# Mixer input normalised once, its products copied out by ScalarE, and the low part of the mixer's weights made in VectorE's stream beside its chains

## The chip, the cores and the metric

The kernel runs on one core of a Trainium2 chip. The metric is the device time of one execution in microseconds. The time before is 1730.99 us, the median of three runs (1728.68 to 1732.05). The profile shows one execution with a span of 1730.2 us.

## The reference

One decoder layer for 512 prompt tokens and 32 sample tokens (8 sequences of 4), 544 rows in all, in float32:

```python
x = x + 0.5 * swiglu(rms(x, norm_ffn1), w_ffn1_gu, w_ffn1_down)     # 1024 -> 2 x 2816 -> 1024
h = rms(x, norm_mix)
qa, ka, va, qkv_b, z_b, b_b, a_b, gate = split(h @ w_in)            # 3 x 1536, 3072, 1024, 8, 8, 2048
o_a, kv_rows = dilated_window_attention(qa, ka, va, caches)         # 12 heads, 3 groups, merged to 4 x 128
o_b, conv_new, s_new = gated_deltanet(qkv_b, z_b, b_b, a_b, ...)    # conv of width 4, 8 heads, chunks
gt = sigmoid(gate)
x = x + (gt[:, :1024] * (o_a @ w_proj_a) + gt[:, 1024:] * (o_b @ w_proj_b)) @ w_out
x = x + 0.5 * swiglu(rms(x, norm_ffn2), w_ffn2_gu, w_ffn2_down)
y = rms(x, norm_out)

def rms(x, w): return x * rsqrt(mean(x * x) + 1e-6) * w
```

The new keys and values, the conv state and the delta-rule state are outputs as well.

## The kernel before

Activations lie transposed: 128 features on the partitions, 544 tokens in two halves of 272 along the row (`NH`). Every large product runs in three passes of a reduced float32: a weight tile is split into a high part (`G`, a rounded copy) and a low part (what the rounding left), the activations likewise (`xh` and `xl`), and hi x hi, hi x lo and lo x hi are summed in PSUM. A *unit* is one 128-column tile of a weight matrix for one half of the tokens; it has eight (or 4, or 11) weight tiles, 24 matmuls of 272 columns. `make_plan` lists all 458 units in order: first feed-forward, the mixer's input projection (`ba`, `gdn`, `at`, `z`, `gate`, 154 units), output projections (`pa`, `pb`, `wo`), second feed-forward.

Before a unit, `prefetch` (L457) lets `split_next` (L424) bring weight tiles in, four at a time: ScalarE makes the high part, and the low part is a subtraction on VectorE or GpSimd. In the mixer it is GpSimd unless the unit's kind is in `LOV`. Four such groups have a place, that is two columns of tiles: while one column is used by its two halves, the next is made. The raw weights come by DMA into two buffers, issued in the mixer from GpSimd's queue (`load_raw`, L401). After a unit's matmuls `kernel_units` (L650) issues its evacuation: the product lies in one of three PSUM banks (`mm`) and must be copied out before the third unit after it.

A norm's weight is multiplied in before the split (`xw_tile`), but a token's 1/rms is not: it is known late, and each evacuation multiplies the product by it (`R(h)`, a tile per half). In `u_gdn`, `u_at`, `u_z` and `u_gate` this is a VectorE product of PSUM and `r`; for two of the three attention groups it also reorders the tokens by residue (strided).

Beside the units run *side chains*, Python generators: the conv (`conv`), the delta-rule pairs (`gdn_pair`), attention slots and so on. Between the matmuls of a unit `pump` (L616) issues the next step of every chain that seems ready. It judges this by `Meter` (L46), an estimate of when each engine gets through what it was given. So the order on every engine is fixed when the program is built, and each engine's queue runs in order. On the chip a VectorE instruction of a chain and an evacuation wait for each other only by their place in that queue.

Tiles come from a pool of 62 (`S`); a chain waits, in the order of issue, until it has enough.

Of the kernel before, what the change touches and what calls it, by code (L numbers as in the profile page):

```python
# [10 lines left out]
F32 = mybir.dt.float32  # L11
F32R = mybir.dt.float32r
# [25 lines left out]
CFG = dict(S=62, S2=4, G=4, G2=8, RAW=2, U3=3, H=10, HM=6, LA=4, LAG=3.0, SLACK=0.0, BANKS=3, PRE=3, LOV=("pa", "pb"), CV=0, WARM=4, EP=8, DUE=2, RES=0, RQ="gpsimd")  # L38
# [87 lines left out]
class Plan:  # L126
    """Order in which the 128 x 128 weight tiles are used; host and chip follow it."""
# [76 lines left out]
def consts():  # L204
    """Arrays that depend on shapes alone: identity, masks and distances."""
# [53 lines left out]
class Builder:  # L259
# [30 lines left out]
    def until(self, ok):  # L290
        """The side chains go on until something holds."""
# [96 lines left out]
    def rsqrt(self, out, v, tmp, steps):  # L388
        """out = v ** -0.5 by a shifted exponent and Newton steps."""
# [34 lines left out]
    def split_next(self, ui, pool=None):  # L424
        """Bring the next group of weight tiles in as hi + lo if a slot is free."""
# [121 lines left out]
    def xw_tile(self, n, h, which):  # L547
        """x * w as hi + lo; the tokens' 1/rms is applied to the products."""
# [9 lines left out]

    def norm_fin(self, h):
        """1/rms of one half of the tokens, on all partitions."""  # L560
# [6 lines left out]
        self.r[h] = self.sp.tile([P, NH], F32, tag="r", name=self.nm("r"), bufs=2)  # L567
# [31 lines left out]
    def step(self, g):  # L599
        """One step of a side chain; it says what its next step waits for."""  # L600
# [15 lines left out]
    def pump(self):  # L616
        """Issue what the side chains have ready."""
# [116 lines left out]

    def enter_mix(self):
# [4 lines left out]
        self.in_mix = True  # L740
        self.live = 16 + 1 + 2 + KT
# [28 lines left out]
    def u_z(self, n, h, wids):  # L770
# [6 lines left out]
        def evac():  # L777
# [5 lines left out]
            self.tt(z, ps, self.R(h), ALU.mult)  # L783
            self.act(t, z, AF.Tanh, scale=0.5)
# [3 lines left out]
    def z_fin(self, n, h, z, t):  # L788
        """A head's output, gated, as hi + lo."""
# [13 lines left out]
    def z_load(self, n):  # L803
        """The output of head n, once it is there."""
# [8 lines left out]
    def fin_a(self):  # L813
        """The attention's heads as hi + lo."""
# [18 lines left out]

    def u_gdn(self, hd, t, h, wids):
        nc = self.nc
        ps = self.unit(wids, self.xn, h)

        def evac():
            ct = t * 8 + hd
            if h == 0:  # L840
# [6 lines left out]
                self.tt(U[:, 3:275], ps, self.R(h), ALU.mult)  # L847
# [3 lines left out]
            self.tt(U[:, 275:515], ps[:, :240], self.R(h)[:, :240], ALU.mult)  # L851
# [942 lines left out]
```

## Time and profile before

| what | value |
|---|---|
| median of the runs | 1730.99 us |
| span of the profiled execution | 1730.2 us |
| TensorE busy | 1656.1 us (96%) |
| VectorE busy | 1072.3 us (62%) |
| ScalarE busy | 573.1 us (33%) |
| GpSimd busy | 373.4 us (22%) |
| chain that ended last | TensorE 73%, VectorE 20%, DMA 3%, ScalarE 2% |

The mixer's units stand at about 415 to 1150 us. In rows of the profile PE is TensorE, DVE VectorE, ACT ScalarE, POOL GpSimd. `mm` and `sd` are PSUM tiles of units and side chains (outside the mixer units use both). Matmuls are pipelined, so a busy PE need not be at its peak. Nearly all instructions carry the line of one helper (L120), so groups are told apart by their tiles' names: `G` weights, `raw` weights as loaded, `U` and `y` input and output of the conv, `av` a projected attention head, `smp` its sample rows, `r` the 1/rms, `Yc`, `Uc` and `inv` a chain's triangular solve, `R` its decay.

### The profile page before, as it was taken

To read this page: it belongs to the slowest core of one execution; us is meant where nothing else is said; L and a number is where in the kernel's file an instruction comes from. 1 tells how busy PE (TensorE), PEld (TensorE's weight loads), DVE (VectorE), ACT (ScalarE), POOL (GpSimd) and SP (SyncE) were. 2 spreads that over 40 slices of the span, in tenths; PEclk is the share of its full clock that TensorE was granted. 3 is DMA by queue.
4 is the path that set the end of the run, shared out by engine and by line. 5 is a ranking of instruction groups with operands and counts; after the bars stand their busy time and mean duration, and the time that the engine had idled before them with its cause. 6 is when DMAs were issued, how large, how long until landed. Compare 5 with 4: busy or idle time off the path is not lost.

```text
span 1730.2 us, 33573 instructions
## 1 busy us (share of the span) xinstructions
PE 1656.1 (96%) x13373; PEld 1607.8 (93%) x13373; DVE 1072.3 (62%) x2508; ACT 573.1 (33%) x1356; POOL 373.4 (22%) x441
## 2 busy tenths in 40 slices
PE   8999999999988999999899899999999999999997
PEld 7999999999988888888889788999999999999996
DVE  7754255545879869789958665344456654255534
ACT  5332223332332324343333244333233323223332
POOL 5000000011545534454425233420011000000012
PEclk9999999999999999999999999999999999999999
DMA  5223222322333455446347666332243222223221
GB/s 177 87 85 98 86 86 86 98 85 75 111 100 115 135 180 185 135 156 193 117 137 238 171 219 182 123 119 89 86 139 97 84 89 87 97 74 98 86 75 63
DMA packets 116434, 205.13 MB, mean 119 GB/s; under 512 B 30962, under 2 KB 57108, under 8 KB 116276
## 3 DMA queue, kind: packets, MB, share of 16 engines
q1 hardware_dynamic: 104708, 162.43, 29.2%
q0 software_dynamic: 10992, 39.99, 7.7%
q8 instruction: 105, 1.72, 0.4%
q10 hardware_dynamic: 576, 0.56, 0.1%
q14 instruction: 53, 0.43, 0.1%
HBM read 172.20 MB, written 30.73 MB: 117 GB/s over the span
## 4 chain that ended last, share of the span: by engine, by line
PE 73%; DVE 20%; DMA 3%; ACT 2%; issue 2%; SPq 1%; POOL 0%; DVEq 0%; ACTq 0%
PE sd L120 40%; PE mm L120 32%; DVE y L120 4%; DVE Yc L120 3%; DVE inv L120 2%; DVE H L120 1%; DVE nrm L120 1%; DVE ast L120 1%; DVE av L120 1%; DVE s L120 1%; DVE R L120 1%; DMA md<-ast 1%; DVE U L120 1%; DVE kq L120 1%; DVE r L120 1%
## 5 line engine op out<-in xcount | busy, mean ns | idle before, releaser
L120 PE MATMUL mm<-xh,G 128*128 128x272 f32 x3632 | 753.7, 297 | 21.6 <-DVE smp L120 10.4
L120 PEld LDWEIGHTS mm<-xh,G 128*128 128x128 f32 x3632 | 596.6, 192 | 42.5 <-issue 26.5
L120 PE MATMUL mm<-xl,G 128*128 128x272 f32 x1816 | 530.0, 292 | 0.5 <-DVE xl L120 0.4
L120 PE MATMUL sd<-xh,G 128*128 128x272 f32 x1904 | 363.4, 288 | 0.0
L120 PEld LDWEIGHTS mm<-xl,G 128*128 128x128 f32 x1816 | 349.2, 192 | 1.4 <-DVE xl L120 0.6
L120 ACT ACTIVATE G<-raw 128x512 fp32r<-128x512 f32 x474 | 273.3, 619 | 178.6 <-PE mm L120 111.6
L120 PEld LDWEIGHTS sd<-xh,G 128*128 128x128 f32 x1904 | 300.5, 188 | 0.2
L120 POOL TENSOR_TENSOR G<-raw,G 128x512 fp32r<-128x512 f32 x158 | 217.3, 1391 | 322.7 <-ACT G L120 303.0
L120 PE MATMUL sd<-xl,G 128*128 128x272 f32 x952 | 273.8, 288 | 0.0
L120 DVE TENSOR_TENSOR G<-raw,G 128x512 fp32r<-128x512 f32 x316 | 204.7, 690 | 70.9 <-ACT G L120 66.7
L120 POOL TENSOR_TENSOR acc<-acc,H 128x272 f32<-128x272 f32 x55 | 44.7, 814 | 911.5 <-ACT H L120 908.1
L120 PEld LDWEIGHTS sd<-xl,G 128*128 128x128 f32 x952 | 179.0, 188 | 0.1
L120 PE MATMUL sd<-hh,G 128*128 128x272 f32 x1287 | 163.0, 288 | 0.0
L120 PEld LDWEIGHTS sd<-hh,G 128*128 128x128 f32 x1287 | 161.8, 188 | 0.1
L120 ACT ACTIVATE H<-H 128x272 f32<-128x272 f32 (+1 forms) x105 | 45.1, 429 | 193.4 <-DVE H L120 193.4
L120 ACT ACTIVATE hh<-H 128x272 fp32r<-128x272 f32 x88 | 38.0, 431 | 202.0 <-DVE H L120 202.0
L120 PE MATMUL mm<-hh,G 128*128 128x272 f32 x825 | 104.7, 288 | 0.0
L120 PEld LDWEIGHTS mm<-hh,G 128*128 128x128 f32 x825 | 103.8, 188 | 0.0
L120 DVE SCALAR_TENSOR_TENSOR y<-U,vec,y 128x568 f32<-128x568 f32 x72 | 94.2, 1308 | 7.8 <-ACT y L120 6.0
L120 DVE SCALAR_TENSOR_TENSOR H<-H,H 128x272 f32<-128x272 f32 x120 | 55.2, 460 | 26.3 <-ACT H L120 25.8
L120 DVE SCALAR_TENSOR_TENSOR x<-sd,x 128x272 f32<-128x272 f32 x49 | 21.4, 439 | 77.9 <-PE sd L120 77.9
L120 DVE TENSOR_TENSOR hh<-H,hh 128x272 fp32r<-128x272 f32 x88 | 38.9, 442 | 43.8 <-ACT hh L120 43.8
(257 smaller groups left out, 1853.3 us busy)
## 6 DMA issues: line engine op xcount, KB each, us to landing
raw<-in_W_dram SPq DMA_DIRECT2D x161, 512.0 KB, 3.6
raw<-in_W_dram POOLq DMA_DIRECT2D x76, 512.0 KB, 4.0
qkv<-qd SPq DMA_DIRECT2D x36, 256.0 KB, 5.4
st<-in_ssm_dram SPq DMA_DIRECT2D x32, 256.0 KB, 4.5
cache<-in_kc_dram SPq DMA_DIRECT2D x28, 256.0 KB, 5.2
cache<-in_vc_dram SPq DMA_DIRECT2D x28, 256.0 KB, 4.3
qd<-av SPq DMA_DIRECT2D x24, 256.0 KB, 4.2
out_dram<-av SPq DMA_DIRECT2D x24, 256.0 KB, 3.8
```

The lines of the kernel that those rows point to most:

```text
L120: r = f(*args, **kw)
```

## The change

`LOV` now has every kind of unit, so all low parts of the mixer are VectorE subtractions. The 1/rms of both halves lies in one tile `rr`. When the second half's is there, a side chain `renorm` makes x * w * r for eight tiles and splits it anew into `xh` and `xl`. From the eleventh unit of the mixer on (`NORMED` = 10) the units use these, and their products need no factor, so `take` copies them out with ScalarE. `u_z` and `u_gate` take ScalarE for their products throughout. The spill of the residual waits for `renorm`. (Docstrings and comments also go, which moves line numbers by two: L120 is L122.)

```diff
-CFG = dict(..., LOV=("pa", "pb"), ...)
+NORMED = 10
+CFG = dict(..., LOV=("pa", "pb", "ba", "z", "gate", "gdn", "at"), ...)
...
+    def renorm(self):
+        ts = []
+        def finish():
+            t, (hi, lo) = ts.pop(0), self.xn2[-1 - len(ts)]
+            self.tt(lo, t, hi, ALU.subtract)
+            self.free(1)
+        for n in range(KT):
+            yield from self.need(3)
+            t = self.S(name="xt")
+            self.stt(t, self.x[n], self.wn[1][:, n:n + 1], self.rr, ALU.mult, ALU.mult)
+            if ts:
+                finish()
+            yield "scalar"
+            self.xn2.append((self.S(dt=F32R, name="xh"), self.S(dt=F32R, name="xl")))
+            self.act(self.xn2[-1][0], t, AF.Copy)
+            ts.append(t)
+            t = None
+            yield "vector"
+        finish()
+        self.renormed = True
...
-        self.r[h] = self.sp.tile([P, NH], F32, tag="r", name=self.nm("r"), bufs=2)
+        if h == 0:
+            self.rr = self.sp.tile([P, NT], F32, tag="r", name=self.nm("r"), bufs=1)
+        self.r[h] = self.rr[:, self.sl(h)]
...
+        elif h == 1 and self.in_mix:
+            self.spawn(self.renorm())
...
             self.prefetch(ui)
+            if ui == first_ba + NORMED:
+                self.until(lambda: self.renormed)
+                self.xn, self.xn2, self.normed = self.xn2, None, True
+                self.free(2 * KT)
...
-            self.tt(z, ps, self.R(h), ALU.mult)
-            self.act(t, z, AF.Tanh, scale=0.5)
+            self.act(t, ps, AF.Tanh, scale=0.5)
+            self.act(z, ps, AF.Copy)
...
+    def take(self, out, ps, r, done):
+        if done:
+            self.act(out, ps, AF.Copy)
+        else:
+            self.tt(out, ps, r, ALU.mult)
...
-                self.tt(U[:, 3:275], ps, self.R(h), ALU.mult)
+                self.take(U[:, 3:275], ps, self.R(h), done)
...
-            self.tt(self.smp[:, t, j, g, :], ps[:, 240:272], self.R(h)[:, 240:272], ALU.mult)
+            self.take(self.smp[:, t, j, g, :], ps[:, 240:272], self.R(h)[:, 240:272], done)
...
-            self.tt(t, ps, self.R(h), ALU.mult)
-            self.act(t, t, AF.Tanh, scale=0.5)
+            self.act(t, ps, AF.Tanh, scale=0.5)
```

On VectorE, at the first `gdn` units of the mixer, stands before (`U` is a unit's product on its way into the conv, `LB` and `LA` the decay's inputs, `y` the conv):

```order
457 L120 TENSOR_TENSOR U_4762<-mm_4737,r_4633 128x272
458 L120 COPY LB_4778<-sd_4773 128x32
459 L120 COPY LA_4779<-sd_4773 128x32
460 L120 TENSOR_TENSOR U_4762<-mm_4766,r_4720 128x240
461 L120 TENSOR_TENSOR U_4762<-mm_4766,r_4720 128x8x4
462 L120 SCALAR_TENSOR_TENSOR y_4816<-U_4762,vec_79,y_4816 128x568 x3
463 L120 MEMSET U_4856 128x3
464 L120 COPY U_4856<-convout_4653 128x8x3
465 L120 TENSOR_TENSOR U_4856<-mm_4826,r_4633 128x272
```

and now:

```order
459 L122 TENSOR_TENSOR U_4760<-mm_4735,r_4632 128x272
460 L122 SCALAR_TENSOR_TENSOR xt_4768<-x_71,vec_79,r_4632 128x544
461 L122 COPY LB_4778<-sd_4773 128x32
462 L122 COPY LA_4779<-sd_4773 128x32
463 L122 TENSOR_TENSOR U_4760<-mm_4764,r_4632 128x240
464 L122 TENSOR_TENSOR U_4760<-mm_4764,r_4632 128x8x4
465 L122 SCALAR_TENSOR_TENSOR xt_4811<-x_72,vec_79,r_4632 128x544
466 L122 TENSOR_TENSOR xl_4801<-xt_4768,xh_4800 128x544
467 L122 TENSOR_TENSOR G_4818<-raw_4460,G_4818 128x512
468 L122 TENSOR_TENSOR G_4821<-raw_4460,G_4821 128x512
469 L122 SCALAR_TENSOR_TENSOR y_4816<-U_4760,vec_79,y_4816 128x568 x3
```

Two subtractions of `G` now stand between two columns' evacuations, and a pair of `xt` and `xl` between a few of the chain's instructions.

On VectorE, a dozen units later, at the first attention head, stands before (`kq`, `scat` and `vT` are the conv's results):

```order
523 L120 TENSOR_TENSOR U_5213<-mm_5217,r_4720 128x8x4
524 L120 TENSOR_TENSOR av_5285<-mm_5259,r_4633 128x272
525 L120 SCALAR_TENSOR_TENSOR kq_5208<-U_5116,y_5223 128x256
526 L120 SCALAR_TENSOR_TENSOR kq_5209<-U_5116,y_5223 128x256
527 L120 SCALAR_TENSOR_TENSOR scat_4656<-U_5116,y_5223 128x32
528 L120 SCALAR_TENSOR_TENSOR y_5292<-U_5213,vec_79,y_5292 128x568 x3
529 L120 TENSOR_TENSOR av_5285<-mm_5294,r_4720 128x240
530 L120 TENSOR_TENSOR smp_4657<-mm_5294,r_4720 128x32
531 L120 SCALAR_TENSOR_TENSOR vT_5350<-U_5213,y_5292 128x512
```

and now:

```order
548 L122 MEMSET U_5266 128x3
549 L122 COPY U_5266<-convout_4652 128x8x3
550 L122 TENSOR_TENSOR G_5298<-raw_5086,G_5298 128x512
551 L122 TENSOR_TENSOR G_5301<-raw_5086,G_5301 128x512
552 L122 SCALAR_TENSOR_TENSOR kq_5119<-U_5173,y_5228 128x256
553 L122 SCALAR_TENSOR_TENSOR kq_5120<-U_5173,y_5228 128x256
554 L122 SCALAR_TENSOR_TENSOR scat_4655<-U_5173,y_5228 128x32
555 L122 SCALAR_TENSOR_TENSOR y_5315<-U_5266,vec_79,y_5315 128x568 x3
556 L122 TENSOR_TENSOR G_5371<-raw_5236,G_5371 128x512
557 L122 TENSOR_TENSOR G_5374<-raw_5236,G_5374 128x512
558 L122 SCALAR_TENSOR_TENSOR vT_5387<-U_5266,y_5315 128x512
```

The copies of `av`, `smp` and `U` are gone from between the conv's instructions, and a pair of `G` has come before every new column.

On ScalarE at the same place stands before:

```order
319 L120 ACTIVATE y_5223<-U_5116,vec_79 128x568
320 L120 ACTIVATE G_5251<-raw_5077 128x512
321 L120 ACTIVATE G_5254<-raw_5077 128x512
322 L120 ACTIVATE U_5116<-y_5223 128x568
323 L120 ACTIVATE y_5292<-U_5213,vec_79 128x568
324 L120 ACTIVATE G_5325<-raw_5180 128x512
325 L120 ACTIVATE G_5328<-raw_5180 128x512
326 L120 ACTIVATE U_5213<-y_5292 128x568
```

and now:

```order
332 L122 ACTIVATE U_5173<-y_5228 128x568
333 L122 ACTIVATE U_5266<-mm_5270 128x240
334 L122 ACTIVATE U_5266<-mm_5270 128x8x4
335 L122 ACTIVATE G_5298<-raw_5086 128x512
336 L122 ACTIVATE G_5301<-raw_5086 128x512
337 L122 ACTIVATE y_5315<-U_5266,vec_79 128x568
338 L122 ACTIVATE av_5338<-mm_5306 128x272
339 L122 ACTIVATE av_5338<-mm_5340 128x240
340 L122 ACTIVATE smp_4656<-mm_5340 128x32
341 L122 ACTIVATE G_5371<-raw_5236 128x512
342 L122 ACTIVATE G_5374<-raw_5236 128x512
343 L122 ACTIVATE U_5266<-y_5315 128x568
```

The evacuations have come into ScalarE's queue, each behind whatever the chains put there, such as the `tanh` (`U` from `y`) that waits for VectorE's three `y`.

## Rows read from the trace of the kernel before

**Rows 1.** Table of stretches: us, busy time of each engine, granted clock, DMA share, GB/s.
```profile
414.00:600.00 186.00, 166.38 (x1249) 161.86 (x1249) 154.17 (x381) 56.02 (x153) 88.92 (x102) 0.94 0.34 110
600.00:800.00 200.00, 188.08 (x1608) 173.51 (x1607) 165.38 (x461) 76.97 (x218) 87.53 (x111) 0.98 0.56 174
800.00:1000.00 200.00, 183.63 (x1628) 167.75 (x1626) 153.57 (x450) 63.31 (x177) 81.31 (x98) 0.97 0.52 163
1000.00:1107.00 107.00, 101.89 (x872) 93.01 (x873) 58.31 (x153) 42.12 (x113) 36.70 (x40) 0.97 0.61 188
```

**Rows 2.** Waits of TensorE, 414 to 1107 us: us in total, times, longest.
```profile
PE mm L120 <- DVE smp L120: 10.4, 3, 5.1
...
PE sd L120 <- DVE nrm L120: 1.1, 1, 1.1
```

**Rows 3.** The chain that ended last: its shares in 414 to 1107 us, and one piece.
```profile
by line: PE mm L120 22.6%; PE sd L120 17.1%; DVE y L120 9.7%; DVE Yc L120 7.0%; DVE inv L120 6.1%; issue 3.8%; DVE nrm L120 2.7%; DVE ast L120 2.3%; DVE av L120 2.1%; DVE s L120 1.9%; DVE R L120 1.9%; DMA md<-ast 1.8%; DVE U L120 1.8%; DVE 
...
1107.14 38.41 PE mm L120 x306
```

**Rows 4.** Timeline of VectorE: start, us, instruction, how many merged, idle before.
```profile
420.84 0.76 DVE L120 SCALAR_TENSOR_TENSOR xl<-x,vec,xh 128x272 fp32r<-128x272 f32 x1 [0.97 <-ACT xh L120]
...
434.11 4.32 DVE L120 SCALAR_TENSOR_TENSOR y<-U,vec,y 128x568 f32<-128x568 f32 x3 [0.90 <-ACT y L120]
...
528.93 0.42 DVE L120 TENSOR_TENSOR Yc<-Yc,inv 128x248 f32<-128x248 f32 x1
...
533.49 1.70 DVE L120 TENSOR_TENSOR Yc<-Yc,inv 128x224 f32<-128x224 f32 x1
...
664.75 2.49 DVE L120 SCALAR_TENSOR_TENSOR y<-U,vec,y 128x568 f32<-128x568 f32 x3
...
1089.52 0.78 DVE L120 TENSOR_TENSOR ol<-H,oh 128x272 fp32r<-128x272 f32 x1 [0.78 <-ACT oh L120]
```

**Rows 5.** Timeline of GpSimd from 533 us.
```profile
533.65 2.66 POOL L120 TENSOR_TENSOR G<-raw,G 128x512 fp32r<-128x512 f32 x2
```

**Rows 6.** Groups of the whole span: busy us, mean ns, idle before.
```profile
L120 PE MATMUL mm<-xh,G 128*128 128x272 f32 x3632 | 753.7, 297 | 21.6 <-DVE smp L120 10.4 <-ACT G L120 5.2 <-DVE av L120 3.2
...
L120 DVE TENSOR_TENSOR G<-raw,G 128x512 fp32r<-128x512 f32 x316 | 204.7, 690 | 70.9 <-ACT G L120 66.7
...
L120 POOL TENSOR_TENSOR G<-raw,G 128x512 fp32r<-128x512 f32 x158 | 217.3, 1391 | 322.7 <-ACT G L120 303.0 <-PE sd L120 19.3
...
L120 DVE SCALAR_TENSOR_TENSOR y<-U,vec,y 128x568 f32<-128x568 f32 x72 | 94.2, 1308 | 7.8 <-ACT y L120 6.0
```

**Rows 7.** ScalarE's group for the weights' high part, 414 to 1107 us.
```profile
L120 ACT ACTIVATE G<-raw 128x512 fp32r<-128x512 f32 x138 | 80.8, 621 | 77.7 <-PE mm L120 65.4 <-DMA raw<-in_W_dram 4.5 <-issue 3.5
```

**Rows 8.** VectorE's groups of product copies, whole span.
```profile
L120 DVE TENSOR_TENSOR av<-mm,r 128x272 f32<-128x272 f32 x36 | 20.4, 567 | 5.3 <-issue 2.8 <-PE mm L120 2.4
...
L120 DVE TENSOR_TENSOR av<-mm,r 128x240 f32<-128x240 f32 x36 | 18.7, 520 | 7.7 <-PE mm L120 7.7
...
L120 DVE TENSOR_TENSOR U<-mm,r 128x272 f32<-128x272 f32 x24 | 10.4, 433 | 1.6 <-PE mm L120 1.6
...
L120 DVE TENSOR_TENSOR U<-mm,r 128x240 f32<-128x240 f32 x24 | 9.5, 397 | 5.9 <-PE mm L120 5.9
...
L120 DVE TENSOR_TENSOR gate<-mm,r 128x272 f32<-128x272 f32 x22 | 9.7, 440 | 36.9 <-PE mm L120 36.9
...
L120 DVE TENSOR_TENSOR smp<-mm,r 128x32 f32<-128x32 f32 x36 | 6.5, 182 | 0.0
```

**Rows 9.** ScalarE's copies out of PSUM, by width.
```profile
L120 ACT ACTIVATE pT<-sd 128x384 f32<-128x384 f32 x8 | 3.9, 486 | 8.5 <-PE sd L120 8.4
...
L120 ACT ACTIVATE vn<-sd 128x512 f32<-128x512 f32 x12 | 7.1, 593 | 11.8 <-PE sd L120 11.5
```

**Rows 10.** Waits of ScalarE for VectorE, 414 to 1107 us.
```profile
ACT U L120 <- DVE y L120: 44.0, 14, 4.2
...
ACT ast L120 <- DVE ast L120: 26.5, 4, 9.8
```

More of the change, by code (lines that the diff above doesn't have):

```diff
@@ L36 @@
 C_KA, C_VA, C_QKV, C_Z, C_B, C_A, C_GATE = 1536, 3072, 4608, 7680, 8704, 8712, 8720
-CFG = dict(S=62, S2=4, G=4, G2=8, RAW=2, U3=3, H=10, HM=6, LA=4, LAG=3.0, SLACK=0.0, BANKS=3, PRE=3, LOV=("pa", "pb"), CV=0, WARM=4, EP=8, DUE=2, RES=0, RQ="gpsimd")
+NORMED = 10
+CFG = dict(S=62, S2=4, G=4, G2=8, RAW=2, U3=3, H=10, HM=6, LA=4, LAG=3.0, SLACK=0.0, BANKS=3, PRE=3, LOV=("pa", "pb", "ba", "z", "gate", "gdn", "at"), CV=0, WARM=4, EP=8, DUE=2, RES=0, RQ="gpsimd")
 MIX_ORDER = [("p", 0), ("p", 1), ("a", 0), ("p", 2), ("a", 1), ("p", 3), ("a", 2), ("a", 3), ("p", 4), ("a", 4), ("p", 5), ("a", 5)]
@@ L654, in kernel_units @@
         pend = []
+        first_ba = next(i for i, u in enumerate(self.units) if u[0] == "ba")
         for ui, u in enumerate(self.units):
             self.prefetch(ui)
+            if ui == first_ba + NORMED:
+                self.until(lambda: self.renormed)
+                self.xn, self.xn2, self.normed = self.xn2, None, True
+                self.free(2 * KT)
             pend.append(getattr(self, "u_" + u[0])(*u[1:]))
@@ L832, in fin_a @@
             self.split(hl[0][:, NPR:NT], hl[1][:, NPR:NT], self.smo[:, 32 * j:32 * j + 32])
+    def take(self, out, ps, r, done):
[3 more added lines that the diff above has]
+            self.tt(out, ps, r, ALU.mult)
     def u_gdn(self, hd, t, h, wids):
-        nc = self.nc
+        nc, done = self.nc, self.normed
         ps = self.unit(wids, self.xn, h)
@@ L850, in evac @@
             us = U[:, 515:571].rearrange("p (b s) -> p b s", s=7)
-            self.tt(U[:, 275:515], ps[:, :240], self.R(h)[:, :240], ALU.mult)
+            self.take(U[:, 275:515], ps[:, :240], self.R(h)[:, :240], done)
             b4 = lambda a: a.rearrange("p (b s) -> p b s", s=4)
-            self.tt(us[:, :, 3:7], b4(ps[:, 240:272]), b4(self.R(h)[:, 240:272]), ALU.mult)
+            self.take(us[:, :, 3:7], b4(ps[:, 240:272]), b4(self.R(h)[:, 240:272]), done)
             self.spawn(self.conv(U, hd, t, self.convs[1]))
@@ L902, in spill @@
         self.xd = self.D([P, KT, NT], "xd")
+        while not self.renormed:
+            yield "w"
         while self.x:
@@ L1362, in u_at @@
     def u_at(self, j, g, t, h, wids):
-        nc, A = self.nc, self.A
+        nc, A, done = self.nc, self.A, self.normed
         ps = self.unit(wids, self.xn, h)
@@ L1372, in evac @@
             if g == 0:
-                self.tt(self.av.rearrange("p a b -> p (a b)")[:, lo:lo + w], ps[:, :w], r, ALU.mult)
+                self.take(self.av.rearrange("p a b -> p (a b)")[:, lo:lo + w], ps[:, :w], r, done)
             else:
                 rn = lambda a: a.rearrange("p (n r) -> p r n", r=4)
-                self.tt(self.av[:, :, lo // 4:(lo + w) // 4], rn(ps[:, :w]), rn(r), ALU.mult)
+                self.take(self.av[:, :, lo // 4:(lo + w) // 4], rn(ps[:, :w]), rn(r), done)
             if h == 0:
                 return
-            self.tt(self.smp[:, t, j, g, :], ps[:, 240:272], self.R(h)[:, 240:272], ALU.mult)
+            self.take(self.smp[:, t, j, g, :], ps[:, 240:272], self.R(h)[:, 240:272], done)
             hd = 4 * g + j
```

1 line of the change is left out of this document (added).

## The prediction

> **What bounds the kernel now.** I read the page first, then a table of stretches, the waits of TensorE, the chain that ended last, and a timeline of VectorE and GpSimd. TensorE is busy nearly always, but its idle time is not spread evenly. In the mixer's part from 414 to 1107 us, 693 us long, four rows of the table [rows 1] give TensorE 640.0 us busy, so 53 us idle. Their granted clock, weighted by length, is 0.965. TensorE's clock has two levels, 1.2 and 2.4 GHz, so 0.965 means that 7% of the 693 us, some 48 us, ran at the lower one, which costs half of that, 24 us. These 53 + 24 = 77 us are what a change to the other engines could win here. It is a little too low, since a matmul counts as busy for 0.297 us [rows 6] though the next may start earlier: each stop hides some tenths.
>
> VectorE is the engine behind this. It is busy 154.2 + 165.4 + 153.6 + 58.3 = 531 us of the 693 [rows 1], 81% up to 1000 us. TensorE's longest waits name its copy of a product (`smp`, up to 5.1 us at once) [rows 2]; twelve such lines of waits for VectorE, from 10.4 to 1.1 us, come to 36 of the 53 us. On the chain that ended last, VectorE's named shares for this stretch (y, Yc, inv, nrm, ast, av, s, R, U) add up to 35.5%, or 246 us [rows 3].
>
> Much of VectorE's time there is not work. Three `y` instructions in a row took 4.32 us in one place and 2.49 in another [rows 4]. A `Yc` that starts at 533.49 takes 1.70 us and lies over two subtractions of `G` that GpSimd runs from 533.65 on [rows 5]; one at 528.93, a little larger and with no such neighbour, takes 0.42 [rows 4]. I compared every VectorE instruction between 414 and 1107 us that a GpSimd subtraction of `G` overlaps with the median of its own kind outside such an overlap (the strided `av` left aside). 101 of them were longer by over 0.15 us, by 95 us in all; the first (`xl`) and the last (`ol`) stand in [rows 4].
>
> The Trainium skill, SBUF — State Buffer, section "Who interferes with whom", says that a VectorE instruction with two SBUF inputs and a GpSimd instruction that reads SBUF lock each other out for a whole instruction. By that rule all 95 us go with the subtractions; if 4.32 us were simply what three `y` cost, none would (rival C).
>
> **The change part by part**, for 414 to 1107 us.
>
> 1. Low part of the weights off GpSimd. 152 subtractions move from GpSimd, where one takes 1.39 us, to VectorE, where one takes 0.690 [rows 6]. 138 of them lie in this stretch (ScalarE's high parts, one for each, are counted there in [rows 7]), which is +95 us for VectorE. What the 101 instructions lose to such overlaps goes: -95 us. `zm`, `kn` and `vk` stay on GpSimd, so a little overlap stays. GpSimd's own time was off the path and wins nothing.
>
> 2. Products copied by ScalarE. VectorE loses 36 + 36 `av` (20.4 + 18.7 us), 36 `smp` (6.5), 20 of 24 `U` pairs (10.4 + 9.5 us, so 16.6, and 20 small third ones at `smp`'s 0.18, 3.6), 32 `gate` and, of the same size, 16 `H` at 0.44 (21.1) [rows 8]: 87 us, of which 7 are gates beside the output projections, where TensorE never waits. That leaves -80 us. ScalarE gains some 60: a 272-wide copy out of PSUM is not in the trace, but 384 columns take 0.486 us and 512 take 0.593 [rows 9], so 272 is about 0.39 on the same line. For the strided `av` I know no ScalarE row; the bounds are 0.39 and VectorE's ratio for it (0.567 as a mean against 0.433 for `U`), so 0.39 to 0.51. I take 0.42, nearer to the first, since a third of the `av` are not strided. ScalarE is busy 238 us of the 693 [rows 1], so it has room by sum.
>
> The Trainium skill, ScalarE: Activation LUTs, section "Rules for kernel authors", speaks against this step: it wants simple arithmetic on VectorE rather than ScalarE. Here both need about 0.4 us for such a tile, so by the rows the move is free where ScalarE has room; by the rule it would be a loss on ScalarE, which nothing in this stretch is bound by.
>
> 3. The normalised input. Eight `xt` (a two-input instruction over 544 columns; `y` over 568 is 2.49 / 3 = 0.83 without an overlap, so 0.80) and eight `xl` (0.690 at 512, so 0.73): 8 x 1.53 = +12 us on VectorE, plus eight copies on ScalarE. All must be done before the eleventh unit of the mixer. Until then TensorE has ten units of 24 matmuls, which at 38.41 us for 306 in a row [rows 3] is 30 us, and VectorE's queue now holds, by the order, eight `xt`/`xl` pairs, ten `G`, four to five `y` triples and the first copies: roughly 12 + 7 + 11 + 8 = 38 us. I count the 12 us as lying fully on the path. The residual's spill (SP queue) starts some 30 us later and is needed only after the mixer: nothing. Sixteen more tiles are held till then, which delays the first delta-rule pair by a few units; by the order the last side matmuls stand before the same unit as now, so I take nothing.
>
> 4. New queues. A copy now stands in ScalarE's queue behind side work that waits for VectorE (`U<-y`, then `U<-mm`), and VectorE's `G` stands behind ScalarE's `G`, which waits for TensorE to let go of a slot: 65 us in all [rows 7]. A weight slot and a PSUM bank are both wanted two units, 6 us, later, so most of these waits are covered; what they cost if not is rival A. GpSimd's raw loads now wait for VectorE instead of GpSimd, a pair of units ahead: nothing.
>
> VectorE's sum is -95 - 80 + 95 + 12 = -68 us: 463 instead of 531. On time, I count each term by how much of it lies on the chain. `y` is the largest part of the 95 us, and 67 of its 94 us are on the chain (9.7% of 693, [rows 3, 6]), so -95 x 0.7 = -66. Copies on the chain: `av` 2.1% and `U` 1.8%, -27. `G` on VectorE only counts while VectorE is the chain: 246 of 531, so 95 x 0.46 = +44. `xt`/`xl` +12. Together -37. The lower clock came after such stops; if half of it goes, -12. The total is -49 us. The span of the profiled execution is 1730.2, the median of the runs 1730.99, 0.8 above; 1731 - 49 = 1682 us.
>
> **Rivals.**
> - A, slower: ScalarE's queue becomes the serial path. Everything that TensorE wants next (weights' high part, then through VectorE the low part, and the emptied bank) stands behind ScalarE's waits for VectorE. In the trace these are long (`U` for `y` 44.0 us, `ast` for `ast` 26.5 with one of 9.8 [rows 10]), and 9.8 is over the 6 us of cover. For it: two engines must now be on time instead of one of three. Against it: these waits are for instructions that the overlaps stretched. If these 44 + 26.5 = 70 us stay and 70% of them reaches TensorE, the 49 us are gone, and from there on the kernel is slower; if all 70 do, the time is 1731 - 49 + 70 = 1752.
> - B, little won: what bounds is then the next thing on the chain, DMA round trips and the order. `md`'s round trip alone holds 1.8% of the chain, 12 us [rows 3], and the order, not readiness, places the side matmuls. If these take two thirds of the 49, 1715. For it: from 1000 to 1107 us VectorE is 54% busy, and the granted clock is 0.97 there too [rows 1]. Against it: only a seventh of the stretch is like that.
> - C, the change doesn't do what it says, as the long `y` have another cause: VectorE then has -80 + 95 + 12 = +27 us, and the path -27 + 44 + 12 = +29: 1760. [Rows 4, 5] speak against it: same instruction, same sizes, 0.83 and 1.44 us each.
> - D, more: VectorE falls so far (67%) that TensorE hardly waits, and the 77 us nearly all go: 1655.
>
> **How the numbers follow.** The forecast, with its own range of 1660 to 1705, has 0.55; D 0.17; B 0.16; A 0.08; C 0.04. The range has to hold 8 in 10: from 1645 (D, with some of the hidden tenths per stop) up to 1720 (most of B); outside are A and C and a rest of B and D. About 0.2% is what a measurement of this kernel can tell from no change, here 3.5 us. Faster by more: 0.55 + 0.17 + most of B = 0.84. Within it: 0.04, out of B. Slower: A and C, 0.12.
>
> **What the profile of the changed kernel would show.** Right: three `y` at about 2.5 us everywhere, and VectorE's `G` at 0.69; VectorE busy near 463 us in the mixer, which is then near 645 us long; the lines "PE mm <- DVE smp" and "<- DVE av" gone; a stop of up to some 12 us before the eleventh unit; a granted clock of 0.98 or more. Wrong: waits of TensorE for VectorE's or ScalarE's `G`, or for ScalarE's `av`, of tens of us (A); `y` still near 1.3 us on average (C); VectorE under 70% busy but TensorE idle for DMA (B). The stretch up to 414 us and that after the mixer should keep their lengths within 2 us.

## The result, and the profile after

The changed kernel takes 1716.7 us (median of 4 runs, 1715.5 to 1718.3) beside 1731.5 for the kernel before on the same chip. The ratio on record is 0.990, 95% interval 0.988 to 0.992 (the two medians alone give 0.991). It is faster by 15 to 17 us: inside the range, but the forecast was 49. The profiled execution spans 1716.5 us.

First the two places in which the forecast's mechanism is to be seen. These are groups of the whole span, columns as in [rows 6]:

```profile
L122 PE MATMUL mm<-xh,G 128*128 128x272 f32 x3632 | 744.3, 296 | 9.0 <-ACT xh L122 3.1
...
L122 DVE TENSOR_TENSOR G<-raw,G 128x512 fp32r<-128x512 f32 x468 | 303.9, 691 | 180.3 <-ACT G L122 174.7
...
L122 DVE SCALAR_TENSOR_TENSOR y<-U,vec,y 128x568 f32<-128x568 f32 x72 | 62.1, 863 | 3.8 <-ACT y L122 1.9
```

`y` fell from 1308 ns to 863 [rows 6], and VectorE's `G` kept its 691, as forecast. The chain's shares from 414 us to the end of the side work (1095 us now) say the same, beside [rows 3]:

```profile
by line: PE mm L122 48.4%; PE sd L122 21.6%; DVE R L122 2.6%; DMA md<-ast 2.4%; DVE y L122 2.3%; issue 2.3%; DMA ob<-od 1.7%; DVE G L122 1.7%; DMA st<-in_ssm_dram 1.5%; DMA cache<-in_kc_dram 1.3%; ACT s L122 1.1%; DVE H L122 0.8%; DMA ast<-
```

VectorE has nearly left the chain: `y` 2.3% where it was 9.7, `Yc` and `inv` gone from the part of the list that is shown. TensorE holds 70% of it. Yet the time hardly moved. The stretches, beside [rows 1], with two short ones below them:

```profile
414.00:600.00 186.00, 169.54 (x1278) 164.62 (x1277) 141.91 (x395) 74.54 (x217) 31.37 (x63) 0.94 0.38 120
600.00:800.00 200.00, 185.96 (x1618) 169.03 (x1617) 147.04 (x444) 87.69 (x267) 35.34 (x70) 0.95 0.54 167
800.00:1000.00 200.00, 187.65 (x1679) 175.20 (x1677) 132.07 (x409) 79.29 (x243) 30.92 (x62) 0.97 0.56 174
1000.00:1107.00 107.00, 103.04 (x866) 95.40 (x867) 58.33 (x178) 48.59 (x138) 11.41 (x19) 0.94 0.57 177
...
450.00:478.00 28.00, 15.18 (x70) 12.79 (x69) 19.99 (x55) 8.01 (x17) 3.95 (x6) 0.63 0.12 39
...
985.00:1010.00 25.00, 14.35 (x118) 12.72 (x118) 15.28 (x46) 4.45 (x12) 4.81 (x6) 0.59 0.64 176
```

VectorE is busy 479 us of the 693 (531 before, 463 forecast). TensorE is idle 47 us instead of 53, and its mean granted clock fell from 0.965 to 0.951. The last two rows show where: in two stops, 53 us together, TensorE is busy 29.5 us at a mean clock of about 0.6. Its waits from 414 to 1095 us, beside [rows 2]:

```profile
PE mm L122 <- DVE xl L122: 8.5, 5, 4.5
PE sd L122 <- DVE X L122: 8.4, 2, 8.0
...
PE mm L122 <- ACT xh L122: 3.1, 2, 1.8
```

VectorE's `smp` and `av` are gone from this list, as forecast. `xl`, the low part of the normalised input, and one `X` of 8.0 us head it, and its high part `xh` stands in it too. **The first stop** is the eleventh mixer unit, the first on the normalised input. TensorE there (start us, us, instruction, idle before and its releaser):

```profile
453.45 0.39 PE L122 MATMUL mm<-xl,G 128*128 128x272 f32 x1 [0.66 <-DVE xl L122]
...
455.77 0.39 PE L122 MATMUL mm<-xh,G 128*128 128x272 f32 x1 [1.80 <-ACT xh L122]
460.69 0.59 PE L122 MATMUL mm<-xl,G 128*128 128x272 f32 x1 [4.53 <-DVE xl L122]
...
467.40 0.60 PE L122 MATMUL mm<-xl,G 128*128 128x272 f32 x1 [2.80 <-DVE xl L122]
...
469.80 1.87 PE L122 MATMUL sd<-g,mats 128*128 128x32 f32 x8 [1.57 <-DVE g L122]
```

and VectorE's timeline, which has no gap longer than 0.7 us from 440 to 470 us:

```profile
457.91 1.29 DVE L122 TENSOR_TENSOR G<-raw,G 128x512 fp32r<-128x512 f32 x2
...
459.22 0.78 DVE L122 SCALAR_TENSOR_TENSOR xt<-x,vec,r 128x544 f32<-128x544 f32 x1
459.92 0.72 DVE L122 TENSOR_TENSOR xl<-xt,xh 128x544 fp32r<-128x544 f32 x1
...
463.42 2.50 DVE L122 SCALAR_TENSOR_TENSOR y<-U,vec,y 128x568 f32<-128x568 f32 x3
...
466.63 0.72 DVE L122 TENSOR_TENSOR xl<-xt,xh 128x544 fp32r<-128x544 f32 x1
```

The eight `xt`/`xl` pairs are spread among `G`, `y` and the decay's small steps, and each `xl` is awaited at once. From the start of its first matmul to the start of its last the unit takes 21.1 us, in the kernel before 5.9, a stop of 15 us in all. From 456 to 477 us TensorE runs at the lower of its two clocks (1.2 GHz): the mean of 0.63 over the 28 us means 21 us of it.

**The second stop** is at the first z units. The first z unit begins at 976.4 us, before at 1021.5, 45 us later. Not all of this is a lead. Here are TensorE's side matmuls (`sd`) from 414 us to the first z unit and from there to the projections, first of the kernel before, then of the changed one (us, busy time and count, granted clock, DMA share, GB/s):

```profile
414.00:1021.50 607.50, 185.69 (x1727) 0.97 0.48 149
1021.50:1148.30 126.80, 23.96 (x247) 0.97 0.54 166
...
414.00:976.40 562.40, 160.12 (x1513) 0.96 0.48 151
976.40:1136.40 160.00, 51.44 (x460) 0.93 0.55 169
```

Some 26 us of side work have only been put behind the first z unit. And the z units need the heads, while the last delta-rule pair has just reached its level stage, which joins the blocks of its triangular solve (`X,B`, `Y,Pm`, `Y,Q`). From 982.6 to 1004.2 us the order holds nothing but side matmuls. TensorE:

```profile
988.91 0.77 PE L122 MATMUL sd<-zm,kf 128*128 128x512 f32 x1
997.71 1.94 PE L122 MATMUL sd<-X,B 128*64 128x64 f32 x16 [8.03 <-DVE X L122]
...
1003.14 1.08 PE L122 MATMUL sd<-cache,pT 128*32 128x128 f32 x16 [0.84 <-DMA cache<-in_vc_dram]
1004.15 0.60 PE L122 MATMUL mm<-xh,G 128*128 128x272 f32 x1
```

and VectorE, which is to make that `X`:

```profile
985.42 1.29 DVE L122 TENSOR_TENSOR G<-raw,G 128x512 fp32r<-128x512 f32 x2 [4.61 <-ACT G L122]
...
988.33 2.57 DVE L122 SCALAR_TENSOR_TENSOR H<-H,H 128x272 f32<-128x272 f32 x1
995.63 0.44 DVE L122 TENSOR_TENSOR H<-H,ob 128x272 f32<-128x272 f32 x1 [4.74 <-DMA ob<-od]
...
997.26 0.30 DVE L122 STREAM_TRANSPOSE X<-Y 32x128 f32<-32x128 f32 x1
```

VectorE stands for 4.7 us at a z unit's product with a head (`ob`) that is still on its way from DRAM, and the `X` that TensorE wants lies behind it. The `H` before it took 2.57 us where the same instruction takes 0.43 at 995.99. It lies over three `zm` that GpSimd still makes: some 2 of the 8 us are what is left of the overlaps.

```profile
987.55 3.03 POOL L122 TENSOR_TENSOR zm<-stk,mats 128x512 fp32r<-128x512 f32 x3
...
995.99 0.43 DVE L122 SCALAR_TENSOR_TENSOR H<-H,H 128x272 f32<-128x272 f32 x1
```

When the projections begin (1136.5 us against 1148.4), 12 of the 45 us are left: 26 were side work put off, and the rest, 7, is about what the stop cost.

### The profile page after: what moved, and what is told of

It reads as the page before. It is cut to its first block, busy times and chain, and to the rows that moved or that the text cites. A ratio compares the mean times of both kernels' runs of the same rounds, so it can differ in the third digit from the quotient of the medians.

```text
span 1716.5 us, 33595 instructions
## 1 busy us (share of the span) xinstructions
PE 1648.8 (96%) x13373; PEld 1603.2 (93%) x13373; DVE 1010.2 (59%) x2460; ACT 618.8 (36%) x1548; POOL 169.0 (10%) x289
## 4 chain that ended last, share of the span: by engine, by line
PE 85%; DVE 7%; DMA 4%; ACT 1%; issue 1%; SPq 0%; DVEq 0%; POOL 0%; ACTq 0%
PE mm L122 43%; PE sd L122 42%; DVE R L122 1%; DMA md<-ast 1%; DVE H L122 1%; DVE y L122 1%; DMA ob<-od 1%; DVE G L122 1%; DMA st<-in_ssm_dram 1%; DVE xl L122 1%; DVE r L122 1%; DMA cache<-in_kc_dram 0%; ACT s L122 0%; SPq L122 0%; DMA raw<-in_W_dram 0%
## 5 line engine op out<-in xcount | busy, mean ns | idle before, releaser
L122 PE MATMUL mm<-xh,G 128*128 128x272 f32 x3632 | 744.3, 296 | 9.0 <-ACT xh L122 3.1
L122 PEld LDWEIGHTS mm<-xh,G 128*128 128x128 f32 x3632 | 590.8, 191 | 27.8 <-issue 13.2
L122 PE MATMUL mm<-xl,G 128*128 128x272 f32 x1816 | 527.6, 291 | 8.5 <-DVE xl L122 8.5
L122 DVE TENSOR_TENSOR G<-raw,G 128x512 fp32r<-128x512 f32 x468 | 303.9, 691 | 180.3 <-ACT G L122 174.7
L122 PE MATMUL sd<-xh,G 128*128 128x272 f32 x1904 | 362.5, 288 | 0.0
L122 PEld LDWEIGHTS mm<-xl,G 128*128 128x128 f32 x1816 | 347.0, 191 | 10.5 <-DVE xl L122 9.8
L122 ACT ACTIVATE G<-raw 128x512 fp32r<-128x512 f32 x474 | 272.1, 622 | 101.5 <-PE mm L122 47.3
L122 PEld LDWEIGHTS sd<-xh,G 128*128 128x128 f32 x1904 | 300.2, 188 | 0.2
L122 PE MATMUL sd<-xl,G 128*128 128x272 f32 x952 | 273.6, 287 | 0.0
L122 PEld LDWEIGHTS sd<-xl,G 128*128 128x128 f32 x952 | 179.0, 188 | 0.1
L122 PE MATMUL sd<-hh,G 128*128 128x272 f32 x1287 | 163.2, 288 | 0.0
L122 PEld LDWEIGHTS sd<-hh,G 128*128 128x128 f32 x1287 | 161.9, 188 | 0.1
L122 POOL TENSOR_TENSOR acc<-acc,H 128x272 f32<-128x272 f32 x55 | 44.5, 810 | 909.9 <-ACT H L122 908.9
L122 ACT ACTIVATE hh<-H 128x272 fp32r<-128x272 f32 x88 | 38.0, 432 | 201.8 <-DVE H L122 201.8
L122 PE MATMUL mm<-hh,G 128*128 128x272 f32 x825 | 104.7, 288 | 0.0
L122 PEld LDWEIGHTS mm<-hh,G 128*128 128x128 f32 x825 | 103.8, 188 | 0.0
L122 ACT ACTIVATE H<-H 128x272 f32<-128x272 f32 (+1 forms) x89 | 38.2, 429 | 161.2 <-DVE H L122 161.2
L122 POOL DMA_DIRECT2D raw<-in_W_dram x76 | 41.7, 549 | 519.9 <-DVE G L122 283.1
L122 DVE SCALAR_TENSOR_TENSOR H<-H,H 128x272 f32<-128x272 f32 x120 | 55.7, 465 | 30.7 <-ACT H L122 30.2
L122 DVE SCALAR_TENSOR_TENSOR x<-sd,x 128x272 f32<-128x272 f32 x49 | 21.5, 439 | 78.2 <-PE sd L122 78.2
L122 DVE TENSOR_TENSOR hh<-H,hh 128x272 fp32r<-128x272 f32 x88 | 39.0, 443 | 43.8 <-ACT hh L122 43.8
L122 DVE SCALAR_TENSOR_TENSOR y<-U,vec,y 128x568 f32<-128x568 f32 x72 | 62.1, 863 | 3.8 <-ACT y L122 1.9
```

The lines of the kernel that those rows point to most:

```text
L122: r = f(*args, **kw)
```

## Experiments

The time estimate that orders the side chains turns out to be central: who makes an instruction, and on which engine's clock the estimate books it, can be set apart. In the cuts of code `eng` issues an instruction without booking it, and `note` books one without issuing it. "Order" below means the order in which the code issues side steps between units. Two runs of the same order, as the traces have it, have the same sequence of TensorE's matmuls throughout. Ratios are to the kernel before on the same chip, each with an interval of 0.001 to 0.003 to either side; 0.1% is 1.7 us.

**1. Four parts.** Theory 1: the order issues the chains too late; theory 2: the start of the second normalisation; theory 3: ScalarE's queue, with the copies behind waits.

```diff
low_alone (the kernel before)
-CFG = dict(..., LOV=("pa", "pb"), ...)
+CFG = dict(..., LOV=("pa", "pb", "ba", "z", "gate", "gdn", "at"), ...)
low_gpsimd (the changed kernel)
-CFG = dict(..., LOV=("pa", "pb", "ba", "z", "gate", "gdn", "at"), ...)
+CFG = dict(..., LOV=("pa", "pb"), ...)
unbooked (the changed kernel, split_next)
+        tv = self.nc.t["vector"]
         self.tt(t[:, 1, :], src, t[:, 0, :], ALU.subtract, self.nc.gpsimd if pool else None)
+        if self.in_mix and not pool and self.units[ui][0] not in ("pa", "pb"):
+            self.nc.t["vector"] = tv
norm22 (the changed kernel)
-NORMED = 10
+NORMED = 22
```

> Only the low parts of the mixer's weights go from GpSimd to VectorE; the mixer's input is not normalised again, and VectorE still makes the products times 1/rms. Theory 1 (the time estimate that orders the side chains books 0.6 us of VectorE for each low part and so issues the delta-rule chains later, and the z units then wait for the last of them): by the order the last pair's inverse is now built in units 241 to 248, before in 217 to 239, so PE stops before z by more than the 49 us that the changed kernel shows there: 1730 to 1750 us, no gain although y takes 0.86 us instead of 1.31. Theory 2 (the second normalisation costs 16 us at its start, the rest works as forecast): without it 1695 to 1705 us.

> The changed kernel with the low parts of the mixer's weights back on GpSimd; the input is normalised once and ScalarE copies the products. Theory 1 (late issue of the chains because of VectorE's booked time): the chains are issued as early as in the kernel before (last inverse built at unit 236), the stop at the first z units is under 20 us, y takes 1.3 us again: 1705 to 1720 us, as good as the whole change. Theory 2 (start of the second normalisation is what costs): it keeps that cost and loses the gain of the shorter y: 1735 to 1745 us. Theory 3 (ScalarE's queue with the copies behind waits costs): 1730 us or more, with PE waiting for ScalarE's copies.

> The changed kernel, but the estimate of VectorE's time that orders the side chains does not count the low parts; each engine does the same work. Theory 1: chains are issued up to 9 units earlier (last inverse built at unit 235 to 237 instead of 244), the stop of 49 us at the first z units falls under 20 us: 1685 to 1695 us. Theory 2: the order of the chains does not matter, 1714 to 1720 us. Theory 3 (the time was lost because VectorE is late): chains issued earlier only wait in the queues, 1716 us or more.

> The changed kernel with the switch to the normalised input before the 23rd mixer unit instead of the 11th, so that VectorE's burst of eight times xt and xl has time. Theory 2: the stop of 16 us at the 11th unit goes and stays gone: 1700 to 1704 us. Theory 1: the units run ahead by 16 us and wait for the same chains at z, which are issued at the same units: 1712 to 1718 us, with the stop at z longer by about what the start gained.

Measured: low parts alone 1712.4 us (0.988); low parts left on GpSimd 1737.8 (1.002); not booked 1743.3 (1.006); switch before the 23rd unit 1703.3 (0.983). Theory 1 in that form fell: chains issued earlier cost 27 us, and TensorE then waits for results that are not there (`g` once for 10.8 us, `as` three times for 9.7). The 1743.3 lies above what any of the three theories expected, and the 1712.4 in neither of its ranges: 7 us above theory 2's. What theory 2 says of the start held: with the switch twelve units later the kernel is 0.73% faster, 13 us. The order is nearly the same there (55 of nearly 2000 side matmuls stand at another place between the units' matmuls), the work too, but for twelve units whose products VectorE multiplies. The first of the two stops is gone; this is the later switch's row:

```profile
450.00:478.00 28.00, 26.02 (x197) 24.52 (x196) 26.12 (x69) 11.26 (x19) 4.87 (x12) 1.00 0.26 76
```

TensorE is busy 26 of the 28 us at full clock, against 15 at 0.63. The low parts alone win as much as the whole change (0.988 and 0.990, within the intervals), so the rest of it won nothing. Theory 3 is left to the third set: low_gpsimd fits its range as well as theory 2's.

**2. Engine against order, for the low parts.**

```diff
vec_booked_gp, gp_booked_vec (the kernel before, split_next, in the mixer)
-        self.tt(t[:, 1, :], src, t[:, 0, :], ALU.subtract, self.nc.gpsimd if pool else None)
+        if self.in_mix and self.units[ui][0] not in ("pa", "pb"):
+            a = (t[:, 1, :], src, t[:, 0, :])
+            self.nc.vector.eng.tensor_tensor(*a, op=ALU.subtract)
+            self.nc.note("gpsimd", "tensor_tensor", a, {})
+        else:
+            self.tt(t[:, 1, :], src, t[:, 0, :], ALU.subtract, self.nc.gpsimd if pool else None)
```

This is the first of the two; in the other, GpSimd makes the low part and VectorE's clock is charged.

> The kernel before with the low parts made by VectorE, while the time estimate that orders the side chains still books them on GpSimd: the order of every other instruction is that of the kernel before. With its twin (GpSimd makes them, booked on VectorE), the kernel before (1733.6) and the low parts moved alone (1712.4) it makes a table of two by two: engine against order. Theory 4 (the 21 us of the low parts come from the freed VectorE: y at 0.86 instead of 1.31 us): 1708 to 1718 us in either order. Theory 5 (they come from the later order of the side chains, so that TensorE meets fewer results that are not there yet): no gain in this order, 1733 to 1745 us.

> The kernel before with the low parts on GpSimd as it has them, while the estimate books them on VectorE: the order is that of the low parts moved alone (last inverse built at units 241 to 248 instead of 217 to 239), y stays at 1.3 us. Theory 4 (the engine): 1728 to 1740 us, no gain. Theory 5 (the order): 1712 to 1720 us.

| low parts made by | order of the kernel before | order of low parts alone |
|---|---|---|
| GpSimd | 1 (before) | 1.011 (1749.9 us) |
| VectorE | 0.990 (1714.6 us) | 0.988 (1712.4 us) |

In one order and in the other, VectorE wins: by 1.0% (17 us) and 2.3%. Theory 4, the engine, holds for the gain. The 1749.9 us are 10 above its range: that order costs 1.1% when GpSimd makes the low parts. `y` follows the engine and not the order: 825 and 808 ns where VectorE makes the low parts, 1345 where GpSimd does in the new order. Here is the group in the kernel that differs from the one before in nothing but the engine:

```profile
L120 DVE SCALAR_TENSOR_TENSOR y<-U,vec,y 128x568 f32<-128x568 f32 x72 | 59.4, 825 | 3.9 <-ACT y L120 2.2
```

The Trainium skill, SBUF — State Buffer, section "Who interferes with whom", describes such a lock between VectorE with two SBUF inputs and GpSimd reading; these runs agree (1308 ns to 825).

**3. Copies by VectorE, and gates before z.**

```diff
copies_vec (switch before the 23rd unit, take)
-            self.act(out, ps, AF.Copy)
+            self.nc.vector.tensor_copy(out, ps)
norm22_gates (switch before the 23rd unit); after_gates (the changed kernel)
-MIX_ORDER += [("z", n) for n in range(6)] + [("t", n) for n in range(4)] + [("z", n) for n in (6, 7)]
+MIX_ORDER += [("t", n) for n in range(4)] + [("z", n) for n in range(8)]
```

A later run, copies_vec_gates, has both.

> The changed kernel with the switch before the 23rd unit (1703.3 us), but the products of conv and attention units copied by VectorE, not by ScalarE; z and gates go from PSUM through ScalarE as in the changed kernel. Low parts moved alone took 1712.4, so all else is worth 9 us there. If taking the copies (some 55 us) off VectorE is what gives them, 1710 to 1716 us, with PE waiting for VectorE's smp and av again; if the copies' place is worth nothing, 1700 to 1706 us.

> The changed kernel with the switch before the 23rd unit, and the sixteen gate units of the four output tiles before all z units instead of behind the sixth. If the stop of PE at the first z units, which wait for the last delta-rule pair (in the changed kernel 11 us of stalls at 975 to 1000 us and 20 us at half clock behind them), is a loss of its own, 1685 to 1695 us. If the side chains' work must be done before the projections anyway, so that the stop only moves, 1700 to 1706 us.

Measured 1694.1 us (0.979) and 1695.5 (0.979). The first went against my expectation: with the copies on VectorE it is faster by 0.4% (the intervals just touch), and not slower. But booking them elsewhere had also changed the order, so the second table:

```diff
cpvec_booked_act (switch before the 23rd unit, take)
-            self.act(out, ps, AF.Copy)
+            self.nc.vector.eng.tensor_copy(out, ps)
+            self.nc.note("scalar", "activation", (out, ps), {})
cpact_booked_vec
+            self.nc.scalar.eng.activation(out, ps, AF.Copy)
+            self.nc.note("vector", "tensor_copy", (out, ps), {})
late_low (switch before the 23rd unit, split_next; lows() runs what is kept)
-        self.tt(t[:, 1, :], src, t[:, 0, :], ALU.subtract, self.nc.gpsimd if pool else None)
+        self.low.append((k, low))
...
             pend = pend[n:]
+            self.lows()
```

> Second table of two by two, on the changed kernel with the switch before the 23rd unit: the products are copied by VectorE, but booked on ScalarE, so the order is that of ScalarE's copies (1703.3 us there; copied and booked on VectorE 1694.1). Theory 6 (copies in ScalarE's queue are what costs: ScalarE stands at a copy whose unit is not finished, its high parts of the weights stand behind it, and VectorE's low parts wait for those): 1690 to 1697 us, and VectorE's G waits for ScalarE's G some 40 us instead of 64. Theory 7 (only the order of the side chains differs): 1701 to 1708 us.

> The other corner: ScalarE copies the products, in the order that belongs to VectorE's copies. Theory 6: 1700 to 1708 us, VectorE's G waits over 55 us for ScalarE's. Theory 7: 1691 to 1697 us.

> The switch before the 23rd unit and ScalarE's copies (1703.3 us), with each low part issued to VectorE one unit later than its high part to ScalarE, no longer right behind it; the next raw load goes with it. The order of the side chains changes too (last inverse at unit 238, not 244). Theory 6: VectorE no longer stands at a low part whose high part is not there; its wait of 64 us falls under 30, and the time to 1690 to 1697 us. If that wait costs nothing, since VectorE has room, 1700 to 1708 us.

> Products copied by VectorE (1694.1 us), the switch before the 23rd unit, and the gates of the output tiles before all z units (8 us won beside ScalarE's copies). If the two gains are separate, 1684 to 1689 us; if the gates only hid what ScalarE's copies delayed, 1692 to 1696 us.

| products copied by | order as booked on ScalarE | order as booked on VectorE |
|---|---|---|
| ScalarE | 0.983 (1703.3 us) | 0.976 (1691.5 us) |
| VectorE | 0.989 (1713.7 us) | 0.979 (1694.1 us) |

The order is worth 0.7 to 1.0%, 12 to 17 us. The engine is worth 0.6% in the first order, in ScalarE's favour; the 0.3% of the second is within the intervals. Theory 6 fell: VectorE's wait for ScalarE's `G` did shrink from 64 to 39 us with the copies on VectorE, and the time rose (to 1713.7 us, 6 above theory 7's range too). Issuing the low parts later shrank that wait to 24 us, for 0.979 (1695.1 us), but its order is another one too, so it settles nothing. The gates ahead of z win 8 us in norm22_gates and nothing with VectorE's copies and their order (1696.3 us, 0.979). In the order of VectorE's copies, with ScalarE copying, TensorE has (start us, us, instruction):

```profile
961.68 1.89 PE L122 MATMUL sd<-X,B 128*128 128x64 f32 x16
...
964.47 0.37 PE L122 MATMUL mm<-xh,G 128*128 128x272 f32 x1
...
971.52 1.14 PE L122 MATMUL sd<-Y,Q 64*64 64x64 f32 x16
```

The level stage begins before the first z unit (964.5 us), lies among its matmuls and those of the next, and is over at 973 us; none of its matmuls has a wait. VectorE's wait for `ob` is still there, 10.8 us up to 985.2, but nothing of the level stage stands behind it, and TensorE has units' matmuls till 984.

**4. What was still open.**

```diff
no_renorm (from cpact_booked_vec, renorm)
-            self.stt(t, self.x[n], self.wn[1][:, n:n + 1], self.rr, ALU.mult, ALU.mult)
+            self.nc.note("vector", "scalar_tensor_tensor", (t, self.x[n], self.wn[1][:, n:n + 1], self.rr), {})
...
-                self.xn, self.xn2, self.normed = self.xn2, None, True
+                self.xn2, self.normed = None, True
v_norm34 (from cpact_booked_vec)
-NORMED = 22
+NORMED = 34
renorm_gp (from v_norm34, renorm)
+            self.nc.scalar.eng.activation(t, self.x[n], AF.Copy, scale=self.wn[1][:, n:n + 1])
+            self.nc.gpsimd.eng.tensor_tensor(t, t, self.rr, op=ALU.mult)
...
+            self.nc.gpsimd.eng.tensor_tensor(lo, t, hi, op=ALU.subtract)
```

> The changed kernel as it is (switch before the 11th unit, ScalarE's copies, its order of the side chains), with only the sixteen gate units of the four output tiles moved ahead of all z units. Theory 8 (in this order the last delta-rule pair's final steps stand alone at the first z units, which wait for them: a stop and half clock near 985 to 1010 us): 1706 to 1711 us, as with the switch at the 23rd unit, where the move was worth 8 us. If the 8 us there came by chance of the order, 1714 to 1719 us.

> The kernel with the switch before the 23rd unit, ScalarE's copies and the order that belongs to VectorE's copies (1691.5 us), leaving out the second normalisation: its 24 instructions (eight xt, xh, xl) are not issued but still booked, so that all else keeps its order, and the units from the 23rd on use the input without 1/rms. The 12 us of VectorE's work that the forecast put on the path: 1679 to 1681 us if they are on it here; 1688 to 1693 us if, away from the 11th unit, they lie beside TensorE's work.

> The same kernel (1691.5 us) with the switch before the 35th unit instead of the 23rd; the order of TensorE's side matmuls is the same at the places looked at. If the switch at the 23rd unit still stops TensorE, 1685 to 1689 us; if it costs nothing there any more, 1690 to 1695 us, as six more units' products are multiplied on VectorE.

> The kernel with the switch before the 35th unit (1690.7 us), its order kept, but the second normalisation off VectorE: ScalarE multiplies by the weight, GpSimd by 1/rms, and GpSimd makes the low part. If what the second normalisation costs beside TensorE (10 us by the run that leaves it out) is its 12 us of VectorE's time, 1681 to 1686 us; if GpSimd's two-input instructions hold VectorE up as the weights' low parts did (sixteen of about 1.5 us), 1690 to 1700 us.

The changed kernel with gates before z: 1707.6 us, 0.985, so 0.5% or 9 us faster than as it is. Its row of the stretches at the place of the second stop:

```profile
985.00:1010.00 25.00, 23.49 (x219) 21.81 (x218) 14.59 (x43) 8.35 (x24) 6.02 (x11) 1.00 0.81 230
```

Full clock and 23.5 us busy, where the changed kernel had 14.35 at 0.59. Theory 8 holds. Leaving the second normalisation out: 1681.7 us, 0.970, against 0.976: 0.6%, 10 us (by the intervals, some 5 either way), so its work is on the path even away from the eleventh unit. The two traces show where: the twin falls behind from the fifth mixer unit (1.4 us) to the twentieth (9.6 us), while the `xt` and `xl` run, and 3 us more later. The run takes out ScalarE's eight `xh` as well. The switch at the 35th unit: 1690.7 us, 0.977, no different from the 23rd. On GpSimd, the normalisation makes it slower than that, 1701.8 us (0.981): 0.4% by the ratios, whose intervals just touch, and 10 us by the two traces. Its two GpSimd groups:

```profile
L575 POOL TENSOR_TENSOR xt<-xt,r 128x544 f32<-128x544 f32 x8 | 12.3, 1537 | 7.0 <-DVE r L122 5.5 <-ACT xt L574 1.4
...
L567 POOL TENSOR_TENSOR xl<-xt,xh 128x544 fp32r<-128x544 f32 x8 | 10.8, 1346 | 0.0
```

They take 23 us on GpSimd instead of 12 on VectorE, and they hold VectorE up. Six VectorE instructions that lie over them are longer than the median of their kind by 15.6 us together. One is a small copy, which takes 0.18 us in v_norm34 and here ends with GpSimd's pair (the second and third line are GpSimd's):

```profile
455.94 2.57 DVE L122 COPY U<-convout 128x24 f32<-128x24 f32 x1
...
455.81 1.36 POOL L575 TENSOR_TENSOR xt<-xt,r 128x544 f32<-128x544 f32 x1
457.13 1.33 POOL L567 TENSOR_TENSOR xl<-xt,xh 128x544 fp32r<-128x544 f32 x1
```

TensorE waits 9.4 us for VectorE's `U` between 427 and 495 us, where v_norm34 has 3.3. Lateness for the switch is not the cause: the loss is there (9 us) at the twentieth unit, fifteen units before it.

The fastest versions are the copies by ScalarE in the order booked on VectorE, with the switch before the 23rd or the 35th unit: 1691.5 and 1690.7 us, 2.3 to 2.4% below the kernel before.

## Why the prediction was right in direction and wrong in size

The forecast's terms on the path, and what stands in their place (us, a ratio's difference times 1731):

| term | forecast | measured | from |
|---|---|---|---|
| low parts to VectorE (-66 + 44) | -22 | -17 to -21 | vec_booked_gp, low_alone |
| products off VectorE, z and gates from PSUM, in the better order | -27 | -31 | no_renorm against low_alone, whose order is another |
| second normalisation's work | +12 | +10 | no_renorm against its twin |
| its early switch | in the 12 | +13 | the changed kernel against norm22 |
| order of the side chains | 0 | +12 | the copies' table, ScalarE's row |
| clock | -12 | +10, within the rows above | granted clock |
| sum | -49 | -13 to -17 | measured as a whole: -15 to -17 |

From low_alone on the rows are steps from one kernel to the next, so that their sum comes to the whole is no check of its own. How the -31 and the +12 are shared out depends on which order is taken as the measure: in the changed kernel's own order the two are -19, where -27 was forecast.

- **Right:** the lock between GpSimd's subtractions and VectorE, and what the low parts win (-17 to -21 against -22; its two terms, -66 and +44, were not measured apart). `y` came to 863 ns where 830 was forecast. ScalarE's 272-wide copy takes 393 ns; I had 0.39, and 0.42 for the strided ones, which take 393 too. The stretch up to 414 us and that behind the mixer kept their lengths within 2 us.
- **Wrong, first step:** "I count the 12 us as lying fully on the path" for the second normalisation. The working had 38 us of VectorE's queue before the eleventh unit against 30 us of matmuls, and I let the 12 us stand for both its work and its place. They are two costs: the work was on the path at the later switch too (10 us), and the early one adds a stop of 15 us, partly made good, and its lower clock (13 us). I had announced a stop of up to 12 us at that place, as the same 12 us, and not added it to the work.
- **Wrong, second step:** "by the order the last side matmuls stand before the same unit as now, so I take nothing". The last ones do. But the last pair's level stage moved from units 238 to 240 to unit 244, into the z units (the first is the 243rd), where the order holds 22 us of side matmuls with no unit's matmuls between them. That stop is worth 8 to 9 of the 12 us (the gates moved ahead win them back). The order was changed by the edits themselves, through the engine on which the estimate books them.
- **Wrong, third step:** "if half of it goes, -12" for the clock. Stretches at half clock between 400 and 1100 us sum to 44 us before and 65 in the changed kernel, 10 us lost instead of 12 won: the two new stops have 20.5 us each, more than the short ones that went. With the first stop gone and the second mostly (cpact_booked_vec) they sum to 20.5 us, half of the 44: the term was of the right size, and it hung on the two steps above.
- **Rivals:** B (1715, little won, the order and round trips next) came nearest in time and in part in mechanism: `ob`'s round trip is in the second stop. What it missed is the first stop. A, ScalarE's queue, is what the table of copies speaks against. The Trainium skill, ScalarE: Activation LUTs, "Rules for kernel authors", wants simple arithmetic on VectorE; here ScalarE's copies were 0.6% better in one order and no worse in the other. C fell with `y` at 863 ns; no run reached D.
- **A slip:** the waits of 1.1 us and more for VectorE are thirteen, 37 us, and not twelve with 36; nothing rests on it.
- **Left open:** the order of the low parts alone is 1.1% worse than that of the kernel before with GpSimd, and no worse with VectorE; and of the 12 to 17 us between the two orders of the copies only the stop at z, 8 to 9 us, was located.

## What to carry to other kernels

Where a planner orders work by estimated engine times, moving an instruction to another engine makes two changes; give the estimate the old engine once and the old engine the new estimate once, and the four corners tell which one paid. A one-time preparation has a price for its work and another for its deadline: before counting it as "on the path", compare what its engine has queued ahead of the deadline with the matmuls that are left till then, and move the deadline. When units run ahead, first take off the work that was only put behind them (here 26 of 45 us), and then look for the next thing that they wait for (here the last chain's serial steps at the z units), since part of the gain is given back there.

## What was unexpected in the hardware

- ScalarE copies 128x272 out of PSUM in 393 ns whether the output is strided or not; VectorE's product of the same tile with `r` took 567 ns as a mean [rows 8], about 430 plain and 635 strided, and its one-input copy (copies_vec) 434, strided or not.
- At both stops TensorE went down to 1.2 GHz and came back only 6 to 7 us after the last wait: the first stop's last wait ended at 469.8 us, and 128x272 matmuls follow each other 0.22 us apart until 476.8 and 0.12 after; at the second the last ended at 1003.1, full pace came by 1009.5.
- GpSimd's two-input instructions over 544 columns took 1.54 and 1.35 us where VectorE's took 0.78 and 0.72, and moving them there cost 0.4% although it freed 12 us of VectorE: the six VectorE instructions over them lost 15.6 us, among them copies of 0.18 us that took 2.6 to 2.7.
